# Sharing the buffers of the early modulation transfers group by group, and queueing the later modulation's loads behind them

## The chip, the cores and the metric

The kernel runs on one core of one Trainium2 chip. The metric is the device time of one execution in microseconds (us). The kernel before the change was timed in three runs: 2575.25, 2576.55 and 2578.53, median 2576.55. One further execution was recorded by the profiler.

## The reference: what is computed

The reference is a backbone of two layers over 512 latent tokens and 256 context tokens, with 2048 features and everything in float32. Cut to what matters here:

```
for l in (0, 1):
    mod  = silu(c)     @ w_mod[l] + b_mod[l]      # shift, scale, gate of the latents, 3 x 2048
    cmod = silu(c_ctx) @ w_mod[l] + b_mod[l]      # the same for the context
    h  = rmsnorm(x,  norm_g[l]) * (1 + scale)  + shift
    hc = rmsnorm(cx, norm_g[l]) * (1 + cscale) + cshift
    u, uc = h @ w_in[l], hc @ w_in[l]             # all mixer columns and the gate path
    y  = concat(mixer 1, mixer 2) * silu(gate columns)
    x  = x + gate * (y @ w_o[l])                  # the context likewise in layer 0
out = rmsnorm(x, final_g)
```

Layer 0 mixes with differential attention (A) and windowed attention (B), layer 1 with two others. The modulation is a product of two vectors (c and c_ctx) with a matrix of 48 MB for each layer. Nothing of layer 0 can start before the shift and the scale for its first features are known; the gate of layer 0 and all of the modulation of layer 1 are needed much later.

## The kernel before, in words

The features lie in 16 chunks of 128, k = 0 to 15. One tile holds one chunk of all 768 tokens (`[128, 768]`, float32). The kernel text goes through a scheduler that decides the order on each engine from dependences and costs, so an engine's order isn't the order of the text.

**The start.** The 16 tiles of x are loaded (`xT`), and their common root mean square is `rs0` (a tile `e`). Then comes a loop over eight groups g = 0 to 7, each for two chunks:

- `mod_first(g)` (lines 134 to 153) computes shift and scale for chunks 2g and 2g+1. It loads 4 MB of `wm0[g]` in 11 tiles `mraw0`, ten of 384 KB and one of 256 KB (L140, on SyncE's DMA queue SP). 32 small fp32 matmuls accumulate in a PSUM tile `T` (L144), each with 32 rows of the result. ScalarE copies `T` to `e` (L149), four tiny matmuls with `sel` transpose it (L151), and `mod_finish` (DVE, L125 and L129) adds bias and gain into `modc`.
- `make_h` (L345 to L361) then makes `h` and its remainder `l` for both chunks: `xn` = xT times rs0 (L348, on GpSimd for two chunks of three, otherwise VectorE), `h` by ScalarE (L353), `xn` again and `l` by VectorE (L356, L218). Each float32 value is split in two parts, and three passes of matmuls h·wh, l·wh and h·wl (L278, L279, L281) stand for one product.
- For each chunk four start columns of the input projection (one head's key, query and value of mixer A, and one gate column) are accumulated: 4 columns × 3 passes × (512 latent and 256 context columns) = 24 matmuls. Below, H0 to H15 are these 24 matmuls of the chunks 0 to 15. While the matmuls of group g stand in the text, those of `mod_first(g+1)` are interleaved with them. The weights of the start columns come every fourth chunk: three `wraw` tiles and one in the slot of `macc` (L268), each split to `wh` (ScalarE, L259) and `wl` (VectorE, L218).

**Where the 88 modulation tiles live.** `hslot` takes one of the 32 slots of pool `hT`, which the 32 tiles h and l fill in the end. `slot` takes one of the 11 slots of pool `s3`, in which `sil` (the stationary operand of the modulation matmuls) and xT[2] to xT[11] live; such a slot comes free when an xT tile has been used by `make_h`. Before the change groups 0 to 4 take `hT` and groups 5 to 7 take `s3`:

```
raw = hslot("mraw0", F32) if g < 5 else slot("mraw0")
```

A load waits until its slot is free. All loads stand in one queue on SP, in an order fixed in advance: a load that waits holds up everything behind it.

**The later modulation.** `mod_later` (L155 to L185) computes four chunks of the rest (block b) from eight tiles `mraw` of 512 KB, in two buffers (L163). For each half tile and each of the two vectors VectorE accumulates (L173: macc += mraw·silc, for c), or ScalarE multiplies in place (L170) and GpSimd adds (L171, for c_ctx). So an eight-tile block has 15 of L173 on VectorE, and 15 of L171 on GpSimd. The generator `later()` goes through twelve blocks with two vectors and then four with one; `tick` draws from it as projections proceed. Its first block is b = 8 of layer 0. Its loads carry no order of their own, except those of the last four blocks, which are issued behind `last_x`.

**After the start.** `load_cs(64)` loads the rotation tables cos and sin (L336), behind the last early load (`last_raw`). The value column goes through `ev` (ScalarE, L447 and L448) to a transpose on TensorE (L453); key and query are copied to `r` (ScalarE, L411 and L413), rotated (`rope`: VectorE L401 and L402, GpSimd L403 and L404) and split (L218: kl, qa, qb). The next projections have weights `wraw` of 512 KB, split into two `wh`/`wl` each; the first of them is the key column of the next head, whose result is copied to an `r` as well (called r_1950 in the order below). wl_1977 belongs to the projection after it.

Of the kernel before, what the change touches and what calls it, by code (L numbers as in the profile page):

```python
# [9 lines left out]
F32 = mybir.dt.float32  # L10
# [7 lines left out]
P = 128  # L18
# [23 lines left out]
def trunk_kernel(ctx: ExitStack, tc: tile.TileContext, T):  # L42
# [5 lines left out]
    wp = ctx.enter_context(tc.tile_pool(name="wp", bufs=4))  # L48
# [16 lines left out]
    def slot(name):  # L65
        return sp["s3"].tile([P, TOK], F32, tag="s3", name=name)
# [13 lines left out]
    def hslot(name, dt=F32R):  # L80
        return hp.tile([P, TOK], dt, tag="hT", name=name)
# [40 lines left out]
    def mod_finish(l, k0, nk, src, nv=2):  # L122

        dst = modc[l][:, k0:k0 + nk, 0:nv]
        nc.vector.tensor_tensor(dst, src, bmod[:, 48 * l + k0:48 * l + k0 + nk].unsqueeze(2).broadcast_to([P, nk, nv]),  # L125
                                op=ALU.add)
        if NCH <= k0 < 2 * NCH:
            g0 = V_NG + 16 * l + k0 - NCH
            nc.vector.scalar_tensor_tensor(dst, dst, 1.0, vcol[:, g0:g0 + nk].unsqueeze(2).broadcast_to([P, nk, nv]),  # L129
                                           op0=ALU.add, op1=ALU.mult)  # L130

    last_raw = [None]

    def mod_first(g):

        acc = pst.tile([P, 512], F32, name="T")
        for r0 in range(0, 32, 3):
            n = min(3, 32 - r0)
            raw = hslot("mraw0", F32) if g < 5 else slot("mraw0")
            last_raw[0] = nc.sync.dma_start(raw[:, :n * 256], T["wm0"][g][:, r0 * 256:(r0 + n) * 256])  # L140
            for i in range(n):
                sec, at = divmod(r0 + i, NCH)
                j = at % 4
                nc.tensor.matmul(acc[32 * j:32 * j + 32, 256 * sec:256 * sec + 256], lhsT=sil[:, at, :],  # L144
                                 rhs=raw[:, 256 * i:256 * i + 256], start=(at < 4), stop=(at >= NCH - 4),
                                 tile_position=(0, 32 * j))
            yield
        asb = sp["ep"].tile([P, TOK], F32, name="e")[:, 0:512]
        nc.scalar.copy(asb, acc)  # L149
        for i in range(4):  # L150
            nc.tensor.matmul(acc[:, 2 * i:2 * i + 2], lhsT=asb[:, P * i:P * i + P], rhs=sel, start=True, stop=True)  # L151
        for sec in range(2):
            mod_finish(0, 2 * g + NCH * (1 - sec), 2, acc[:, 4 * sec:4 * sec + 4].rearrange("p (c v) -> p c v", c=2))
        yield

    def mod_later(l, b, nv, behind=None):

        macc = sm.tile([P, 2, 512], F32, name="macc", bufs=1)
        for r in range(8):
            raw = wp.tile([P, 1024], F32, name="mraw", bufs=2)  # L160
            rv = raw.rearrange("p (k c) -> p k c", k=2)
            with tc.issue_after(behind.ins) if behind is not None else nullcontext():
                nc.sync.dma_start(raw, T["wm1"][b + 4 if l else b - 8, r])  # L163
            for i in range(2):
                for v in range(nv):
                    sc = silc[:, 16 * v + 2 * r + i:16 * v + 2 * r + i + 1]
                    if r == 0 and i == 0:
                        nc.scalar.mul(macc[:, v, :], rv[:, i, :], sc)
                    elif v == 1:
                        nc.scalar.mul(rv[:, i, :], rv[:, i, :], sc)  # L170
                        nc.gpsimd.tensor_tensor(macc[:, v, :], macc[:, v, :], rv[:, i, :], op=ALU.add)  # L171
                    else:
                        nc.vector.scalar_tensor_tensor(macc[:, v, :], rv[:, i, :], sc, macc[:, v, :],  # L173
                                                       op0=ALU.mult, op1=ALU.add)
            if r < 7:
                yield
        mp = psj.tile([P, 512], F32, name="J")
        for i in range(4):
            for v in range(nv):
                at = 4 * i + 2 * v  # L180
                nc.tensor.matmul(mp[:, at:at + 2], lhsT=macc[:, v, 128 * i:128 * i + 128],  # L181
                                 rhs=ones[:, 0:2], start=True, stop=True)
        mod_finish(l, 4 * b, 4, mp[:, 0:16].rearrange("p (a v o) -> p a v o", v=2, o=2)[:, :, 0:nv, 0], nv)
        yield
# [13 lines left out]

    def later():
        for b in range(8, 12):  # L200
            yield from mod_later(0, b, 2)
        for b in (4, 5, 6, 7, 0, 1, 2, 3):
            yield from mod_later(1, b, 2)
        for b in range(8, 12):
            yield from mod_later(1, b, 1, last_x)

    bg = later()
    due = [0.0, 0]

# [165 lines left out]
    for _ in mod_first(0):  # L375
        pass
    for g in range(NCH // 2):
# [3 lines left out]
        for k in (2 * g, 2 * g + 1):  # L381
            for i, (lat, cx) in enumerate(start_ps):
                if k % 4 == 0:
                    raw = sm.tile([P, 2, 512], F32, name="macc", bufs=1).rearrange("p a b -> p (a b)") if i == 3 else None
# [657 lines left out]
```

## Time and profile before

| what | value |
|---|---|
| three runs, median (lowest to highest) | 2576.55 us (2575.25 to 2578.53) |
| the profiled execution's own time | 2573.45 us |
| its span in the profile | 2571.7 us |
| mean granted TensorE clock | 0.977 |
| PE busy | 2427.3 us, 94% of the span |
| DVE / ACT / POOL busy | 63% / 44% / 20% |
| 384 KB modulation loads | 80, median 7.3 us from issue to landing |

In the views, PE is TensorE, DVE is VectorE, ACT is ScalarE, POOL is GpSimd, and SPq is SyncE's DMA queue. Timeline rows read: start in us, duration in us, engine, line, operation, out<-in, shapes, count, and in brackets the idle time before with what ended it. Rows of waits read: waiting engine, tile and line, what it waited for, us in total, times, longest. Rows of windows read: from:to, length, then busy us (and instructions) of PE, PEld, DVE, ACT and POOL, the granted TensorE clock, the DMA share and GB/s.

### The profile page before, as it was taken

The numbers are of one execution on the slowest core, as the hardware profiler recorded it, in microseconds if no ns is written. First come the engines' busy times: TensorE is split into PE (matmuls) and PEld (weight loads), VectorE is DVE, ScalarE is ACT, GpSimd is POOL, SyncE is SP. The second block draws the span as 40 slices with busy tenths as digits, with TensorE's granted clock in tenths as the row PEclk, the third lists the DMA queues.
The fourth block names the chain that finished last, engine by engine and source line by source line (L and its number), as shares of the span: only waits on it lengthen the run. The fifth ranks groups of instructions, "written<-read, shape, count | busy, mean of one in ns | idle before, by whom it ended". The sixth has DMA issues, their size and how long they took to land.

```text
span 2571.7 us, 36748 instructions
## 1 busy us (share of the span) xinstructions
PE 2427.3 (94%) x14214; PEld 2088.3 (81%) x14214; DVE 1608.2 (63%) x2720; ACT 1128.6 (44%) x2143; POOL 517.6 (20%) x340
## 2 busy tenths in 40 slices
PE   4889999999999999999999999899999999999998
PEld 2667888988788888878878888688888888887787
DVE  4367666656865787877666554857735325776534
ACT  3244444544554554544343332444434334554434
POOL 1132001101400354353303442310010001000010
PEclk9899999999999999999999999899999999999999
DMA  9762111111312233342334554535522222222234
GB/s 326 251 216 74 48 50 56 56 55 57 105 53 69 90 133 124 107 145 97 118 127 153 183 182 138 205 106 170 178 70 79 78 83 70 62 87 70 92 117 148
DMA packets 99087, 297.51 MB, mean 116 GB/s; under 512 B 11616, under 2 KB 12640, under 8 KB 98912
## 3 DMA queue, kind: packets, MB, share of 16 engines
q1 hardware_dynamic: 98912, 295.16, 34.5%
q8 instruction: 112, 1.84, 0.3%
q14 instruction: 63, 0.52, 0.1%
HBM read 269.16 MB, written 25.95 MB: 115 GB/s over the span
## 4 chain that ended last, share of the span: by engine, by line
PE 51%; DVE 7%; issue 2%; ACT 2%; DMA 2%; POOL 1%; ACTq 0%; SPq 0%; DVEq 0%; POOLq 0%
PE J L278 13%; PE J L279 13%; PE J L281 13%; PE O L533 4%; PE S L477 2%; DVE macc L173 2%; PE T L518 2%; DMA mraw<-in_wm_dram 2%; PE S L473 2%; DVE wl L218 1%; POOL macc L171 1%; DVE l L359 1%; DVE mc L489 1%; PE J L181 1%; PE T L243 0%
## 5 line engine op out<-in xcount | busy, mean ns | idle before, releaser
L278 PE MATMUL J<-h,wh 128*128 128x512 f32 (+1 forms) x2224 | 791.3, 359 | 23.8 <-ACT h L353 13.4
L279 PE MATMUL J<-l,wh 128*128 128x512 f32 (+1 forms) x2224 | 769.0, 356 | 4.7 <-DVE l L359 2.7
L281 PE MATMUL J<-h,wl 128*128 128x512 f32 (+1 forms) x2224 | 709.1, 356 | 2.8 <-DVE wl L218 2.8
L218 DVE TENSOR_TENSOR wl<-wraw,wh 128x512 fp32r<-128x512 f32 x500 | 402.2, 809 | 348.2 <-ACT wh L259 326.6
L259 ACT CAST wh<-wraw 128x512 fp32r<-128x512 f32 x492 | 302.4, 618 | 545.2 <-PE J L279 472.1
L278 PEld LDWEIGHTS J<-h,wh 128*128 128x128 f32 x2224 | 424.7, 192 | 104.7 <-ACT h L353 14.5
L279 PEld LDWEIGHTS J<-l,wh 128*128 128x128 f32 x2224 | 426.1, 192 | 62.6 <-DVE l L218 3.9
L281 PEld LDWEIGHTS J<-h,wl 128*128 128x128 f32 x2224 | 390.6, 192 | 38.8 <-DVE wl L218 5.1
L171 POOL TENSOR_TENSOR macc<-macc,mraw 128x512 f32<-128x512 f32 x180 | 267.9, 1489 | 254.1 <-ACT mraw L170 226.6
L278 PE MATMUL J<-yh,wh 128*128 128x512 f32 (+1 forms) x800 | 276.6, 352 | 5.1 <-ACT yh L441 5.1
L279 PE MATMUL J<-yl,wh 128*128 128x512 f32 (+1 forms) x800 | 272.8, 351 | 1.0 <-DVE yl L218 0.9
L173 DVE SCALAR_TENSOR_TENSOR macc<-mraw,silc,macc 128x512 f32<-128x512 f32 x240 | 241.7, 1007 | 42.3 <-DMA mraw<-in_wm_dram 38.6
L281 PE MATMUL J<-yh,wl 128*128 128x512 f32 (+1 forms) x800 | 253.2, 350 | 0.0
L489 DVE TENSOR_REDUCE mc<-S 128x1 f32<-128x768 f32 (+3 forms) x208 | 166.1, 799 | 137.9 <-PE S L477 88.1
L170 ACT ACTIVATE mraw<-mraw,silc 128x512 f32<-128x512 f32 x180 | 129.4, 723 | 192.4 <-DVE macc L173 171.6
L522 ACT CAST pth<-T 128x256 fp32r<-128x256 f32 (+2 forms) x288 | 124.9, 450 | 160.6 <-PE T L518 157.3
L278 PEld LDWEIGHTS J<-yh,wh 128*128 128x128 f32 x800 | 150.9, 190 | 32.8 <-ACT yh L441 5.9
L279 PEld LDWEIGHTS J<-yl,wh 128*128 128x128 f32 x800 | 151.1, 189 | 22.1 <-DVE yl L218 2.8
L218 DVE TENSOR_TENSOR ptl<-T,pth 128x256 fp32r<-128x256 f32 (+2 forms) x288 | 144.5, 514 | 38.6 <-ACT pth L522 35.1
L498 ACT ACTIVATE e<-S,nb 128x256 f32<-128x256 f32 (+3 forms) x144 | 104.3, 724 | 145.1 <-DVE nb L494 102.2
L281 PEld LDWEIGHTS J<-yh,wl 128*128 128x128 f32 x800 | 140.6, 190 | 12.4
L403 POOL TENSOR_TENSOR r<-r,cos 128x512 f32<-128x512 f32 x31 | 44.3, 1429 | 476.3 <-DVE t L402 361.4
(287 smaller groups left out, 3424.7 us busy)
## 6 DMA issues: line engine op xcount, KB each, us to landing
mraw<-in_wm_dram SPq DMA_DIRECT2D x128, 512.0 KB, 3.7
wraw<-in_ew_dram SPq DMA_DIRECT2D x96, 512.0 KB, 3.6
wraw<-in_ow_dram SPq DMA_DIRECT2D x64, 512.0 KB, 3.6
wraw<-in_wo_dram SPq DMA_DIRECT2D x62, 512.0 KB, 3.8
mraw<-in_wm_dram SPq DMA_DIRECT2D x80, 384.0 KB, 7.3
xT<-in_xT_dram SPq DMA_DIRECT2D x16, 384.0 KB, 7.8
res<-in_xT_dram SPq DMA_DIRECT2D x16, 384.0 KB, 4.4
xad<-nx SPq DMA_DIRECT2D x16, 384.0 KB, 2.3
```

The lines of the kernel that those rows point to most:

```text
L170: nc.scalar.mul(rv[:, i, :], rv[:, i, :], sc)
L171: nc.gpsimd.tensor_tensor(macc[:, v, :], macc[:, v, :], rv[:, i, :], op=ALU.add)
L173: nc.vector.scalar_tensor_tensor(macc[:, v, :], rv[:, i, :], sc, macc[:, v, :], op0=ALU.mult, op1=ALU.add)
L218: nc.vector.tensor_tensor(o, a, h.bitcast(F32), op=ALU.subtract)
L259: nc.scalar.copy(wh[:, :n, :], rv[:, k0:k0 + n, :])
L278: nc.tensor.matmul(o, lhsT=wh, rhs=xh[:, c0:c1], start=first and (opens or o is lat), stop=False)
L279: nc.tensor.matmul(o, lhsT=wh, rhs=xl[:, c0:c1], start=False, stop=False)
L281: nc.tensor.matmul(o, lhsT=wl, rhs=xh[:, c0:c1], start=False, stop=last and (closes or o is lat))
L489: nc.vector.reduce_max(mc, S, axis=AX.X)
L498: nc.scalar.activation(e, S, AF.Exp, bias=nb, scale=scale, accum_out=den)
L522: nc.scalar.copy(ph, tv)
L533: nc.tensor.matmul(o, lhsT=v[:, cols[i]], rhs=pt[part][:, i, :], start=(n == 0), stop=(n == len(steps) - 1))
```

## The change

`mod_first` no longer decides by the group alone. The first 11, 11, 11, 11, 11, 6, 4 and 3 tiles of groups 0 to 7 take `hT`, the rest take `s3`, and the last two tiles of group 7 take the two `mraw` buffers of the later modulation. The later modulation's blocks 8 to 11 of layer 0 and 0 to 7 of layer 1 get `last_raw[0]`, the last early load, as the load behind which theirs are issued. Behind the edit at line 139 all line numbers grow by 7: L144 is L151 then, L151 is L158, L163 is L170, L173 is L180, L218 is L225, L268 is L275, L278 is L285.

```
-            raw = hslot("mraw0", F32) if g < 5 else slot("mraw0")
+
+            i = r0 // 3
+            if i < (11, 11, 11, 11, 11, 6, 4, 3)[g]:
+                raw = hslot("mraw0", F32)
+            elif g == 7 and i > 8:
+                raw = wp.tile([P, 1024], F32, name="mraw", bufs=2)
+            else:
+                raw = slot("mraw0")
             last_raw[0] = nc.sync.dma_start(raw[:, :n * 256], T["wm0"][g][:, r0 * 256:(r0 + n) * 256])
...
         for b in range(8, 12):
-            yield from mod_later(0, b, 2)
+            yield from mod_later(0, b, 2, last_raw[0])
         for b in (4, 5, 6, 7, 0, 1, 2, 3):
-            yield from mod_later(1, b, 2)
+            yield from mod_later(1, b, 2, last_raw[0])
```

The number behind a tile's name tells the instance. Tiles mraw_832 to mraw_912 are group 4's, mraw_968 to mraw_1066 group 5's, mraw_1116 to mraw_1196 group 6's, mraw_1252 to mraw_1350 group 7's.

TensorE, at the end of group 4's modulation matmuls, before:

```order
L144 MATMUL T<-mraw_853,sil 32x256 x3
L144 MATMUL T<-mraw_968,sil 32x256 x3
L144 MATMUL T<-mraw_973,sil 32x256
L144 MATMUL T<-mraw_864,sil 32x256 x3
L144 MATMUL T<-mraw_973,sil 32x256 x2
L144 MATMUL T<-mraw_990,sil 32x256
L144 MATMUL T<-mraw_869,sil 32x256 x3
L144 MATMUL T<-mraw_990,sil 32x256 x2
L144 MATMUL T<-mraw_995,sil 32x256 x3
...
L144 MATMUL T<-mraw_912,sil 32x256 x2
L144 MATMUL T<-mraw_1050,sil 32x256 x3
L151 MATMUL T<-sel,e 128x2 x4
```

The same place now, with the first rows of H8 behind it:

```order
L151 MATMUL T<-mraw_853,sil 32x256 x3
L151 MATMUL T<-mraw_864,sil 32x256 x3
L151 MATMUL T<-mraw_869,sil 32x256 x3
L151 MATMUL T<-mraw_880,sil 32x256 x3
L151 MATMUL T<-mraw_885,sil 32x256 x3
L151 MATMUL T<-mraw_896,sil 32x256 x3
L151 MATMUL T<-mraw_901,sil 32x256 x3
L151 MATMUL T<-mraw_912,sil 32x256 x2
L158 MATMUL T<-sel,e 128x2 x4
L285 MATMUL J<-h_8_945,wh 128x512 x3
```

Group 5's matmuls, 27 of which stood among group 4's and the other five in the first rows of H8, have left this place.

TensorE, around the start of H10 (chunk 10, the first of group 5), before:

```order
L281 MATMUL O<-h_9_954,wl 128x512
L281 MATMUL S<-h_9_954,wl 128x256
L144 MATMUL T<-mraw_1116,sil 32x256 x3
L144 MATMUL T<-mraw_1121,sil 32x256 x3
L278 MATMUL J<-h_10_1099,wh 128x512
```

And now:

```order
L288 MATMUL O<-h_9_954,wl 128x512
L288 MATMUL S<-h_9_954,wl 128x256
L151 MATMUL T<-mraw_1017,sil 32x256 x3
L151 MATMUL T<-mraw_1034,sil 32x256 x3
L151 MATMUL T<-mraw_1039,sil 32x256 x3
L151 MATMUL T<-mraw_1050,sil 32x256 x3
L151 MATMUL T<-mraw_1055,sil 32x256 x3
L151 MATMUL T<-mraw_1066,sil 32x256 x2
L158 MATMUL T<-sel,e 128x2 x4
L285 MATMUL J<-h_10_1099,wh 128x512 x3
```

Group 5's own matmuls, 15 of them among H9's and 17 behind H9, and its `sel` now stand directly ahead of H10; before, its `sel` was inside H9, and group 6's matmuls stood here. In the same way group 7's matmuls, 30 of which stood ahead of H12, now stand at the end of H13, with `sel` directly ahead of H14, and group 6's stand inside H11, with `sel` ahead of H12.

VectorE, from the last early `l` tile (l0_15, chunk 15) to the first rotation, before (macc_2241 belongs to the later modulation's first block, whose tiles are mraw_2242, 2833, 3552, 3971, 4563, 4840, 5566 and 6151):

```order
L173 SCALAR_TENSOR_TENSOR macc_2241<-mraw_4563,silc_181,macc_2241 128x512
L218 TENSOR_TENSOR l0_15_1393<-xn_1390,h0_15_1392 128x768
L173 SCALAR_TENSOR_TENSOR macc_2241<-mraw_4840,silc_181,macc_2241 128x512 x2
L218 TENSOR_TENSOR wl_1837<-wraw_1834,wh_1836 128x512
L401 TENSOR_TENSOR t2_1454<-r_1451,sin64_1449 32x512
```

And now:

```order
L180 SCALAR_TENSOR_TENSOR macc_2241<-mraw_2833,silc_181,macc_2241 128x512
L225 TENSOR_TENSOR l0_15_1393<-xn_1390,h0_15_1392 128x768
L180 SCALAR_TENSOR_TENSOR macc_2241<-mraw_3552,silc_181,macc_2241 128x512
L225 TENSOR_TENSOR wl_1837<-wraw_1834,wh_1836 128x512
L180 SCALAR_TENSOR_TENSOR macc_2241<-mraw_3552,silc_181,macc_2241 128x512
L408 TENSOR_TENSOR t2_1454<-r_1451,sin64_1449 32x512
```

At the first rotation the block stands at its sixth tile of eight before (11 of 15 L173 done), and at its third now (5 of 15 done). Between the first rotation and wl_1977 four L173 stood before (tiles 5566 and 6151); seven stand there now (tiles 3971, 4563, 4840 and the first of 5566).

SP, at the end of the early loads, before: behind group 7's last tile mraw_1350 come cos, sin and six loads of the later modulation; two of its loads stand far ahead, behind the first four weight loads. Now:

```order
L275 DMA macc<-in_ew_dram 128x512
L147 DMA mraw<-in_wm_dram 128x768
L147 DMA mraw<-in_wm_dram 128x512
L343 DMA cos_1447<-in_cos_dram 128x512
L343 DMA sin_1449<-in_sin_dram 128x512
L147 DMA mraw_1034<-in_wm_dram 128x768
```

This is the place of the two early loads of the later modulation: group 7's last two tiles and the tables have taken it. All eight loads of the first later block now stand behind mraw_1274, group 7's third tile, which has become the last early load of the queue.

## The prediction

> **What bounds the kernel now.** I read the page first, then the windows of the first 300 us, then TensorE's timeline there, then those of VectorE and SP. The page says who is the bottleneck:
>
> ```profile
> span 2571.7 us, 36748 instructions
> PE 2427.3 (94%) x14214; PEld 2088.3 (81%) x14214; DVE 1608.2 (63%) x2720; ACT 1128.6 (44%) x2143; POOL 517.6 (20%) x340
> ```
>
> TensorE is idle for 144 us in all. The change touches loads and work of about the first 230 us, so I look at its windows there (PE's busy us is the second number, DVE's the fourth, POOL's the sixth, then clock, DMA share, GB/s):
>
> ```profile
> 105.00:110.00 5.00, 3.82 (x13) 3.15 (x14) 4.05 (x10) 2.50 (x4) 0.00 (x0) 0.66 0.00 0
> 129.00:137.00 8.00, 7.52 (x30) 4.66 (x29) 5.61 (x7) 1.79 (x4) 1.98 (x1) 0.57 1.03 400
> 145.00:160.00 15.00, 15.00 (x108) 9.35 (x108) 4.06 (x6) 3.23 (x6) 2.02 (x2) 1.00 0.90 309
> 160.00:187.00 27.00, 22.78 (x163) 17.59 (x163) 24.09 (x30) 14.83 (x24) 16.38 (x11) 1.00 0.48 152
> 187.00:207.00 20.00, 13.93 (x55) 10.58 (x54) 19.74 (x18) 13.17 (x22) 10.88 (x7) 0.91 0.34 107
> 207.00:222.00 15.00, 11.48 (x70) 11.04 (x71) 14.76 (x17) 4.67 (x8) 6.36 (x4) 0.77 0.22 71
> 222.00:300.00 78.00, 73.38 (x439) 64.90 (x438) 48.22 (x100) 34.97 (x70) 2.60 (x2) 0.98 0.16 53
> ```
>
> Three stretches stand out. From 145 to 160 TensorE has no gap at full clock. From 187 to 222 VectorE is busy 34.5 of 35 us and TensorE idles 9.6. From 222 on TensorE is busy 94% again, so what has been lost by then isn't won back: the shift at about 222 us is the forecast's shift at the end. (A measurement of this kernel tells a difference from none at about 0.2%, 5.15 us.)
>
> Now TensorE's timeline, at the starts of groups 2, 4, 5, 6 and 7 and behind H15:
>
> ```profile
> 81.27 1.92 PE L144 MATMUL T<-mraw,sil 128*32 128x256 f32 x28
> 83.87 1.05 PE L151 MATMUL T<-sel,e 128*128 128x2 f32 x8 [0.69 <-ACT e L149]
> 86.34 1.65 PE L278 MATMUL J<-h,wh 128*128 128x512 f32 x3 [1.42 <-ACT h L353]
> ...
> 106.18 1.22 PE L278 MATMUL J<-h,wh 128*128 128x512 f32 x2 [1.37 <-ACT h L353]
> ...
> 128.57 0.97 PE L278 MATMUL J<-h,wh 128*128 128x512 f32 x3 [1.42 <-ACT h L353]
> ...
> 143.93 0.49 PE L278 MATMUL J<-h,wh 128*128 128x512 f32 x1
> 145.23 0.63 PE L144 MATMUL T<-mraw,sil 128*32 128x256 f32 x6
> 145.79 0.51 PE L278 MATMUL J<-h,wh 128*128 128x512 f32 x1
> ...
> 160.25 3.22 PE L144 MATMUL T<-mraw,sil 128*32 128x256 f32 x52
> 163.40 0.97 PE L278 MATMUL J<-h,wh 128*128 128x512 f32 x3
> 176.35 0.96 PE L278 MATMUL J<-h,wh 128*128 128x512 f32 x3 [1.18 <-ACT h L353]
> 179.39 0.50 PE L279 MATMUL J<-l,wh 128*128 128x512 f32 x1 [1.73 <-DVE l L218]
> 186.73 0.28 PE L281 MATMUL S<-h,wl 128*128 128x256 f32 x1
> 189.53 0.66 PE L453 MATMUL J<-identr,ev 128*128 128x128 f32 x4 [2.51 <-ACT ev L447]
> 204.42 0.39 PE L281 MATMUL J<-h,wl 128*128 128x512 f32 x1
> 210.52 0.58 PE L278 MATMUL J<-h,wh 128*128 128x256 f32 x1 [5.71 <-ACT r L411]
> 218.61 0.40 PE L278 MATMUL J<-h,wh 128*128 128x512 f32 x1
> ```
>
> Between groups lies what I call a tail: from the last modulation matmul of a group (in group 2 at 83.19) over copy, `sel`, `modc` and `h` to the first H matmul (86.34), 3.15 us. It is bare in the early groups. It is covered at H10 and H12, which start without a wait (143.93, 163.40), because the modulation matmuls were done a group earlier and others stand in the tail. After the bare tails of H6 and H8 the clock is low for several us (0.66, 0.57).
>
> **The change, part by part.** The prices of TensorE's work first. From 179.39 to 187.01 run the last 43 of the 48 matmuls of H14 and H15: 7.62 us, so 8.5 for all 48 at full clock. A modulation tile (three matmuls) costs 0.56 us between H matmuls (145.23 to 145.79), and in a block one matmul costs 3.22/26 = 0.124 (52 entries are 26 matmuls, two passes each). A spell at low clock costs 8 us × (1 − 0.57) = 3.4 behind H8; behind H6 5 × (1 − 0.66) = 1.7 in that window alone. I take 2.8.
>
> *Group 4 to 5.* The loads up to group 4 keep their count ahead of them: 9 tiles in `s3` slots and the first 1 MB still come early, only others, and 0.13 MB more (under 0.4 us at 400 GB/s). The first four groups and H8's start I leave at 128.6. There, while TensorE waited for group 4's last tiles, it did 27 of group 5's 32 modulation matmuls. Now they stand among and behind H9. So this group becomes like the early ones: 8.5 (H8, H9) + 2.8 (clock) + 5 × 0.56 + 17 × 0.124 = 4.9 (modulation) + 3.15 (tail) = 19.4. Group 2's cycle, measured, is 106.18 − 86.34 = 19.84. H10 starts at 148.0 instead of 143.93: +4.0. Group 5's first six tiles are now loaded late, behind group 4's and four weight tiles; six tiles at 0.98 us from about 122 are there before H9 needs the first at about 138, so they cost nothing. That 0.98 is 384 KB at the 400 GB/s of the window 129:137.
>
> *Group 5 to 6.* 8.5 + 2.8 (a tail at H10 that wasn't bare) + 4 × 0.56 + 20 × 0.124 = 4.7 + 2.5 (`sel` to h, 83.87 to 86.34; the copy is hidden by 15 matmuls of H11) = 18.5. H12 at 166.5 instead of 163.40: +3.1.
>
> *Group 6 to 7.* 8.5 + 1.4 (half of 2.8, the tail being shorter) + 0.56 + 29 × 0.124 = 4.2 + 3.15 = 17.2. H14 at 183.7 instead of 176.35: +7.4. The load queue could hold group 7's last three tiles here, behind three weight loads of the next projection, which wait for wl (chunks 12 to 15); these are free at about H11's end, 164, and three tiles land by 170, ahead of 175.
>
> *H14 and H15.* 8.5 + 2.8 = 11.3 against 10.66, whose wait for `l` (1.73) now falls under the slower matmuls, as L173 no longer stands ahead of it. H15 ends at 195.0 instead of 187.0: **+8.0**. Ends: +3.7 if only one of the three new tails costs clock, +9.3 if all do in full.
>
> [...] The windows above show clocks of 0.66 and 0.57 after two tails of 3.15 us, in which the only work is 1.05 us of tiny matmuls. [...]
>
> *The later modulation.* Its loads were free runners before, and two landed at 43 us. Now the first is issued when group 7's last tiles are used, about 178. SP, VectorE and GpSimd before:
>
> ```profile
> 33.39 1.31 SPq L163 DMA_DIRECT2D mraw<-in_wm_dram  x2
> ...
> SPq L163 <- POOL macc L171: 38.7, 8, 11.4
> ```
>
> ```profile
> 187.01 1.75 DVE L218 TENSOR_TENSOR wl<-wraw,wh 128x512 fp32r<-128x512 f32 x1 [1.30 <-PE S L281]
> 191.59 0.69 DVE L218 TENSOR_TENSOR wl<-wraw,wh 128x512 fp32r<-128x512 f32 x1
> 208.48 0.75 DVE L173 SCALAR_TENSOR_TENSOR macc<-mraw,silc,macc 128x512 f32<-128x512 f32 x1
> 209.27 0.95 DVE L218 TENSOR_TENSOR qa<-r,qa 64x768 fp32r<-64x768 f32 x1
> 218.09 2.40 DVE L218 TENSOR_TENSOR wl<-wraw,wh 128x512 fp32r<-128x512 f32 x2
> ```
>
> The same subtraction takes 0.69 us alone and 1.75 beside a GpSimd operation: each GpSimd tile costs VectorE about 1.06. From H15's end to wl_1977 (187.0 to 218.1) VectorE works 31.1 us without a break, with four L173 and eight GpSimd operations. In the new order seven L173 stand there, and about eleven GpSimd operations: 3 × 0.75 + 3 × 1.06 = +5.4. In return VectorE is freed of eight L173 before H15's end, where I have counted that already (the wait for `l`). How much of the 5.4 reaches TensorE: before, it resumed at 210.52 and needed 8.1 us to 218.61, when wl_1977 was just coming. In the new order the first scores stand ahead of those matmuls and wait for qa. Qa comes 22.3 to 25 us after H15's end, then 8.1 us: 30.4 to 33.1 after H15's end, against 31.6 before, so −1.2 to +1.5 by this path; by wl_1977 up to +5.4. I take **+2**, nearer to the first path, since TensorE's 8.1 us of matmuls run while VectorE does what stands behind qa.
>
> The 5.71 us that TensorE waited for `r` don't come off this sum: the copy stood behind a multiplication for the last of the eight tiles on ScalarE, and stands behind one for the fifth now, so this wait may go; but qa is awaited in its place, at nearly the same distance from H15's end.
>
> *Moved tables.* cos and sin (512 KB) come early and are in the 0.13 MB above. Nothing more.
>
> Behind 230 us the order differs in places of two or three rows; I price it at 0 ± 3.
>
> Sum: 8.0 + 2 = +10 on the profiled execution's 2573.45 (span 2571.7, 1.75 around it), 2583.5; the median of the runs lies 3.1 above that execution, so **2586.5**.
>
> **The rivals.**
>
> *No change.* TensorE's waits behind H15 (2.51 and 5.71, and the low clock after the second: 0.77 over 15 us, 3.4) swallow the loss. If VectorE keeps up, TensorE goes from H15's end at 195.0 through 17.8 us of matmuls (187.0 to 204.81, with its first wait) to 212.8, and on at full clock, against 210.52: +2.3, less some 2 for the clock: about 0, 2577. For: ScalarE's copy of `r` stands behind fewer tiles. Against: VectorE is busy 98% in 187 to 222, and gets more there. Chance 0.19.
>
> *The clock holds.* [...] For: H14's gap of 1.18 us left it at 1.00 (160 to 187). Against: the two rows above. Chance 0.05.
>
> *Faster.* VectorE, relieved of eight L173 between 160 and 187, gives h and l sooner; the clock holds at H12 and H14 (H15's end +3.7), and the loads of the later modulation fall late enough that VectorE's chain doesn't grow: less 5.71 and 3.4 behind H15: −5.4, 2571. It decides at about 210: TensorE must not wait there. Against: qa. Chance 0.14.
>
> *Much slower.* The later tiles land behind each other (SP waited 38.7 us in eight waits for GpSimd), and weight loads stand behind them in the queue: two waits of the mean, 4.8 each, on top: about +20, 2596. Chance 0.07.
>
> **How the numbers follow.** The forecast (+5.2 to +14) has 0.55. Slower by over 0.2%: 0.55 + 0.07 = 0.62. Within: 0.19 + 0.05 = 0.24. Faster: 0.14. The range leaves out the faster case's lower part and the much slower case's upper: 2573 to 2596. It takes in the ends of H15 (+3.7 to +9.3) with the ends of the VectorE chain (−1.2 to +5.4) and ± 3 behind: 2576 to 2594.
>
> **What would show it.** In the new profile: H8 at 128.6, H10 at 148, H12 at 166.5, H14 at 184, H15's end at 195, each with clock below 0.8 in the 5 us behind; then a wait of TensorE for qa at about 204 to 219, and the match of 218.61 at about 229. I am wrong if H10 starts before 146 (then group 4's cover wasn't worth what I think), or if TensorE has no wait over 2 us between 195 and 225 (then the loss was swallowed).

## The result, and the profile after

| | before | after |
|---|---|---|
| median (lowest to highest), four runs each | 2575.90 us (2571.75 to 2578.53) | 2595.92 us (2593.62 to 2597.11) |
| profiled execution, its span | 2573.45, 2571.7 | 2595.23, 2593.5 |

The ratio is 1.0078, 95% interval 1.0061 to 1.0096: slower by 20.0 us, where +10 was forecast. In a later series (17 runs of before, six of after) the same two kernels stood at 2572.70 and 2589.42, ratio 1.0069, interval 1.0054 to 1.0083: +16.7.

The page of the kernel after, in its first lines:

```profile
span 2593.5 us, 36751 instructions
PE 2433.7 (94%) x14214; PEld 2095.1 (81%) x14214; DVE 1607.9 (62%) x2720; ACT 1128.9 (44%) x2143; POOL 517.3 (20%) x340
```

The same 14214 matmuls were busy 6.4 us longer (the mean granted clock was 0.975 instead of 0.977), and TensorE idled 159.8 us instead of 144.4: 15.4 more. Its timeline shows where the idle time lies. These are its entries at the starts of H8, H10, H12 and H14 and behind H15:

```profile
124.28 1.05 PE L158 MATMUL T<-sel,e 128*128 128x2 f32 x8 [0.74 <-ACT e L156]
126.75 1.13 PE L285 MATMUL J<-h,wh 128*128 128x512 f32 x3 [1.42 <-ACT h L360]
...
144.05 1.05 PE L158 MATMUL T<-sel,e 128*128 128x2 f32 x8 [0.73 <-ACT e L156]
146.52 0.97 PE L285 MATMUL J<-h,wh 128*128 128x512 f32 x3 [1.42 <-ACT h L360]
...
163.32 0.96 PE L285 MATMUL J<-h,wh 128*128 128x512 f32 x3 [1.41 <-ACT h L360]
...
181.82 1.50 PE L285 MATMUL J<-h,wh 128*128 128x512 f32 x3 [1.42 <-ACT h L360]
...
192.65 0.28 PE L288 MATMUL S<-h,wl 128*128 128x256 f32 x1
193.94 0.66 PE L460 MATMUL J<-identr,ev 128*128 128x128 f32 x4 [1.00 <-ACT ev L454]
...
205.44 0.50 PE L288 MATMUL J<-h,wl 128*128 128x512 f32 x1 [1.70 <-DVE wl L225]
...
219.17 0.58 PE L480 MATMUL S<-kh,qa 128*128 128x256 f32 x1 [8.45 <-DVE qa L225]
...
226.93 0.40 PE L285 MATMUL J<-h,wh 128*128 128x512 f32 x1
...
230.91 0.62 PE L288 MATMUL J<-h,wl 128*128 128x512 f32 x2 [2.29 <-DVE wl L225]
```

H10 and H12, which started without a wait, now wait 1.42 and 1.41 us for `h`, at the end of a tail. H15 ends at 192.93 instead of 187.01. The wait of 5.71 for `r` is gone; 8.45 for qa has come, and then 2.29 for wl.

The windows of the same stretch (busy us and count of PE, PEld, DVE, ACT, POOL, then clock, DMA share, GB/s):

```profile
126.70:131.70 5.00, 4.78 (x17) 3.71 (x18) 4.90 (x6) 1.70 (x3) 2.00 (x1) 0.66 0.91 349
131.70:136.70 5.00, 5.00 (x34) 3.33 (x32) 1.18 (x2) 0.00 (x0) 0.00 (x0) 1.00 0.40 132
146.50:151.50 5.00, 4.36 (x15) 3.52 (x16) 4.93 (x6) 1.67 (x3) 2.01 (x1) 0.66 0.98 355
163.30:168.30 5.00, 4.35 (x15) 3.51 (x16) 4.48 (x7) 1.67 (x3) 0.00 (x0) 0.66 0.92 339
181.80:186.80 5.00, 4.98 (x18) 4.05 (x19) 4.97 (x8) 4.22 (x7) 1.35 (x2) 0.66 0.15 61
192.90:218.20 25.30, 13.83 (x55) 10.58 (x54) 24.94 (x22) 14.19 (x23) 15.51 (x10) 0.82 0.32 99
218.20:231.00 12.80, 9.21 (x57) 8.72 (x57) 12.63 (x15) 5.29 (x11) 7.00 (x5) 0.81 0.23 78
```

Behind each tail the clock is 0.66 over the next five us (for 3.41 of them the trace has 0.50), and then 0.99 or 1.00; the second trace of this kernel (after_again, below) has 0.66 or 0.67 behind all four as well. From H15's end to the start of qa VectorE is busy 24.94 of 25.30 us: it is the bound there. Before, the matching stretches were these:

```profile
187.01:209.30 22.29, 13.92 (x55) 10.58 (x54) 21.96 (x21) 13.19 (x23) 10.87 (x7) 0.90 0.35 114
209.30:222.00 12.70, 11.48 (x70) 11.04 (x71) 12.53 (x14) 4.63 (x8) 6.36 (x4) 0.77 0.18 52
```

POOL had 7 and then 4 operations there, and has 10 and 5 now. VectorE's timeline of the kernel after shows some of the later modulation's operations there (L180 is the old L173) and the two results that TensorE waits for:

```profile
198.10 1.76 DVE L180 SCALAR_TENSOR_TENSOR macc<-mraw,silc,macc 128x512 f32<-128x512 f32 x1
...
207.00 2.56 DVE L180 SCALAR_TENSOR_TENSOR macc<-mraw,silc,macc 128x512 f32<-128x512 f32 x2
...
218.17 0.95 DVE L225 TENSOR_TENSOR qa<-r,qa 64x768 fp32r<-64x768 f32 x1
...
220.13 0.75 DVE L180 SCALAR_TENSOR_TENSOR macc<-mraw,silc,macc 128x512 f32<-128x512 f32 x1
...
229.10 3.44 DVE L225 TENSOR_TENSOR wl<-wraw,wh 128x512 fp32r<-128x512 f32 x2
```

From H15's end to the start of wl_1977 it works 36.2 us (192.93 to 229.10), and before 31.1. The match of the old 218.61 stands at 226.93, and TensorE's next matmul with wl at 230.91.

### The profile page after: what moved, and what is told of

Its sections match the earlier page's. It is cut to its first block, busy times and chain, and to the rows that moved or that the text cites. A ratio compares the mean times of both kernels' runs of the same rounds, so it can differ in the third digit from the quotient of the medians.

```text
span 2593.5 us, 36751 instructions
## 1 busy us (share of the span) xinstructions
PE 2433.7 (94%) x14214; PEld 2095.1 (81%) x14214; DVE 1607.9 (62%) x2720; ACT 1128.9 (44%) x2143; POOL 517.3 (20%) x340
## 5 line engine op out<-in xcount | busy, mean ns | idle before, releaser
L285 PE MATMUL J<-h,wh 128*128 128x512 f32 (+1 forms) x2224 | 788.8, 358 | 21.2 <-ACT h L360 15.9
L225 DVE TENSOR_TENSOR wl<-wraw,wh 128x512 fp32r<-128x512 f32 x500 | 398.4, 801 | 340.4 <-ACT wh L266 314.8
L285 PEld LDWEIGHTS J<-h,wh 128*128 128x128 f32 x2224 | 423.9, 191 | 99.6 <-ACT h L360 16.8
L285 PE MATMUL J<-yh,wh 128*128 128x512 f32 (+1 forms) x800 | 276.3, 351 | 5.2 <-ACT yh L448 5.2
L180 DVE SCALAR_TENSOR_TENSOR macc<-mraw,silc,macc 128x512 f32<-128x512 f32 x240 | 247.3, 1030 | 49.4 <-DMA mraw<-in_wm_dram 45.4
L285 PEld LDWEIGHTS J<-yh,wh 128*128 128x128 f32 x800 | 150.7, 189 | 32.8 <-ACT yh L448 6.0
L225 DVE TENSOR_TENSOR ptl<-T,pth 128x256 fp32r<-128x256 f32 (+2 forms) x288 | 144.8, 515 | 39.9 <-ACT pth L529 36.2
L286 PEld LDWEIGHTS J<-yl,wh 128*128 128x128 f32 x800 | 151.1, 189 | 22.5 <-DVE yl L225 3.3
L288 PEld LDWEIGHTS J<-yh,wl 128*128 128x128 f32 x800 | 140.7, 190 | 12.6
```

The source lines that it names most:

```text
L225: nc.vector.tensor_tensor(o, a, h.bitcast(F32), op=ALU.subtract)
L285: nc.tensor.matmul(o, lhsT=wh, rhs=xh[:, c0:c1], start=first and (opens or o is lat), stop=False)
L286: nc.tensor.matmul(o, lhsT=wh, rhs=xl[:, c0:c1], start=False, stop=False)
L288: nc.tensor.matmul(o, lhsT=wl, rhs=xh[:, c0:c1], start=False, stop=last and (closes or o is lat))
```

## The experiments

The prediction's account: the places of the early transfers make the tails (about 8 us at H15's end), and the loads queued behind them lengthen VectorE's chain a little. One rival: the queueing is the larger part, because the first later block (b = 8 of layer 0, "block 8" below) loses a stretch in which it cost little. A second rival: the order of the load queue costs far behind the start. All ratios are against before in the same series.

One measure serves all runs. The trace lists each matmul with its columns; I take the time at which TensorE had done as many columns as in the first trace of before at time t, minus t. The table also has H15's end itself. It leaves out after_warm, whose added matmuls change the columns.

| kernel | H15's end | at 240 | at 400 | at 900 | at 2500 | ratio (95%) |
|---|---|---|---|---|---|---|
| before | 187.0 | 0 | 0 | 0 | 0 | |
| before_again | 183.5 | -3.5 | -3.5 | -3.6 | -5.1 | one run |
| after | 192.9 | 12.1 | 11.6 | 14.3 | 21.8 | 1.0078 (1.0061 to 1.0096) |
| after_again | 193.9 | 13.1 | 12.7 | 16.5 | 14.2 | 1.0069 (1.0054 to 1.0083) |
| queue_only | 188.6 | 7.1 | 11.8 | 12.9 | 11.6 | 1.0049 (1.0037 to 1.0062) |
| place_only | 206.9 | 14.0 | 13.6 | 16.9 | 17.9 | 1.0062 (1.0050 to 1.0075) |
| before_late8 | 183.9 | -8.9 | 9.6 | 10.7 | 12.4 | 1.0053 (1.0039 to 1.0067) |
| after_late8 | 195.2 | 2.4 | 21.0 | 22.5 | 23.4 | 1.0088 (1.0074 to 1.0101) |
| before_spread8 | 182.2 | -9.8 | -9.1 | -6.0 | -4.3 | 0.9992 (0.9983 to 1.0001) |
| after_spread8 | 191.8 | -1.9 | 1.5 | 3.9 | 4.7 | 1.0031 (1.0020 to 1.0042) |
| g5_first | 191.5 | 9.0 | 15.5 | 16.7 | 24.7 | 1.0075 (1.0060 to 1.0090) |
| before_tail2 | 184.9 | -5.4 | -5.1 | -1.7 | -3.4 | 0.9997 (0.9988 to 1.0007) |
| before_l1order | 184.3 | -2.9 | -2.8 | -3.0 | -1.4 | 1.0010 (1.0001 to 1.0020) |

### One part alone

**queue_only**, before with the second part of the change:

```diff
-            yield from mod_later(0, b, 2)
+            yield from mod_later(0, b, 2, last_raw[0])
-            yield from mod_later(1, b, 2)
+            yield from mod_later(1, b, 2, last_raw[0])
```

> Only the second part of the change: the old places of the early tiles (groups 0 to 4 in hT, 5 to 7 in s3), but the later modulation's loads queued behind the last early load. In its order group 5's modulation matmuls stand among group 4's again, and group 6's sel and group 7's matmuls are spread over H9 to H13, as before; six L173 stand between the first rotation and wl_1977 (four before, seven in the changed kernel). Theory (two costs that add: bare tails of groups 5 to 7 before H15's end, then VectorE's longer list to wl_1977): H15 ends at 185 to 188, wl_1977 2 to 4 us later than before, and the whole run is 0 to +5 us against before. Rival A (the queueing alone is the cost, the places nothing): +15 to +20 us. Rival B (the places alone are the cost): 0 +- 3 us and no later wl_1977.

Measured: 2585.29 against 2573.84, +11.4: above the theory's range and below rival A's. H10 and H12 keep their covers. Ahead of H14 TensorE waits 2.16 us instead of 1.18, and the clock behind it is 0.50 for 6.8 us. H15 ends 1.6 us later than in before's first trace. Then two long waits follow on TensorE, and a third much later:

```profile
210.07 0.39 PE L278 MATMUL J<-h,wh 128*128 128x256 f32 x1 [3.62 <-ACT r L411]
...
224.67 1.01 PE L281 MATMUL J<-h,wl 128*128 128x512 f32 x2 [5.25 <-DVE wl L218]
...
384.38 0.58 PE L473 MATMUL S<-kh,qb 128*128 128x256 f32 x1 [4.63 <-ACT e L498]
```

The matmul that waits 5.25 us for wl had no wait in before (219.31). From H15's end to 240 this kernel loses 5.5 us more, with no tail in that stretch: the prediction's +2 for the queueing was too small. The wait of 4.63 for ScalarE's `e` at 384 belongs to another stretch. It stands in the traces of g5_first, before_late8 and after_late8 too (4.6 us each), and in neither of the two traces of before nor the two of after. These four kernels lose 6 to 7 us on before from 340 to 400; why `e` comes late in their orders wasn't followed.

**place_only**, after's table for the slots, without the branch that puts group 7's last tiles into the later modulation's buffers, and without the queueing (shown against after):

```diff
-            elif g == 7 and i > 8:
-                raw = wp.tile([P, 1024], F32, name="mraw", bufs=2)
...
-            yield from mod_later(0, b, 2, last_raw[0])
+            yield from mod_later(0, b, 2)
-            yield from mod_later(1, b, 2, last_raw[0])
+            yield from mod_later(1, b, 2)
```

> Only the first part: the new sharing of hT and s3 (group 7's last two tiles in s3, as the later modulation keeps its two buffers and its own early loads). In its order the modulation matmuls of groups 5 to 7 stand as in the changed kernel, at the end of H9, H11 and H13, and no L173 is left between the first rotation and wl_1977. Theory: H15 ends 5 to 8 us later than before, but VectorE's list behind it is shorter than before by four L173 and some six GpSimd operations, so that the wait of 5.7 us before the context matmuls goes: shift at 230 us -2 to +3, whole run -3 to +5 us. Rival A (the queueing alone): 0. Rival B (the places alone): +12 us or more at 230 us, and +15 to +20 at the end.

Measured: 2590.38 against 2573.84, +16.5. That is the number of rival B, but not its mechanism: H15 ends at 206.9, 14 later than in after. H8 already starts 3.6 us later (130.31 instead of 126.75; TensorE waits longer for its modulation tiles). The rest comes from H12 on, where 14 of block 8's 15 L173 stand ahead of the last `l` tile on VectorE. VectorE waits for block 8's loads four times on the way (8.7 us in all):

```profile
167.11 1.11 PE L283 MATMUL J<-h,wh 128*128 128x512 f32 x3 [2.37 <-ACT h L358]
...
171.77 0.79 PE L284 MATMUL J<-l,wh 128*128 128x512 f32 x1 [2.91 <-DVE l L223]
...
190.88 1.65 PE L283 MATMUL J<-h,wh 128*128 128x512 f32 x3 [3.28 <-ACT h L358]
...
197.12 0.80 PE L284 MATMUL J<-l,wh 128*128 128x512 f32 x1 [3.95 <-DVE l L223]
```

Of these 14 us, 12 are back by 240 (14.0 there against 12.1 in after): the work that stood ahead of H15 doesn't stand behind it. The two parts don't add: by 240 they cost 7.1 and 14.0, and both together 12.1. Both move the same work of block 8 about the same narrow stretch.

### Without the first later block at the start

To see the places without that collision, block 8 is taken out of the start in both orders.

**before_late8 and after_late8**: all loads of block 8 are issued behind the weight load last recorded when its step is drawn (the same edit in both; after has `last_raw[0]` for the other blocks):

```diff
+    last_w = [None]
...
-            yield from mod_later(0, b, 2)
+            yield from mod_later(0, b, 2, last_w[0] if b == 8 else None)
...
-        nc.sync.dma_start(raw[:, :nk * P], w[col // P][:, k0 * P:(k0 + nk) * P])
+        last_w[0] = nc.sync.dma_start(raw[:, :nk * P], w[col // P][:, k0 * P:(k0 + nk) * P])
```

> The kernel before, with the same late first block of the later modulation and nothing else. Theory: H15 ends 1 to 3 us earlier than before (no L173 ahead of the l tiles), the waits of 2.5 and 5.7 us behind it shrink to under 2 in all, so the shift at 230 us is -6 to -10, and the whole run is -10 to -2 us, faster than both kernels. Rival (the work of the block costs the same wherever it stands): 0 +- 3 us.

> The changed kernel, with the first later block's loads held back further, behind the last weight load that stands ahead of it in the text (in head 1), so that no L173 stands ahead of wl_1977; the places as in the changed kernel. Theory: H15's end as in the changed kernel (+5 to +6 on before), no wait for qa (8.4 us in the changed kernel) nor for wl_1977 (2.3): shift at 230 us -3 to +2, at the end -2 to +8 by what the order does at the start of layer 1. Rival (VectorE isn't what makes TensorE wait there, but the late start itself): shift at 230 us stays at +10 to +12.

Measured: 2585.88 and 2595.98 against 2573.84. By 230 us before_late8 is ahead by 9.5. Then the whole block comes in one stretch, and TensorE loses 12 us there. The window of before_late8:

```profile
230.00:260.00 30.00, 22.86 (x125) 19.73 (x124) 26.46 (x38) 16.77 (x31) 17.63 (x12) 0.88 0.36 125
```

And of before:

```profile
230.00:260.00 30.00, 30.00 (x184) 26.52 (x183) 18.09 (x40) 14.25 (x29) 2.60 (x2) 1.00 0.16 56
```

Twelve GpSimd operations instead of two, VectorE at 88% instead of 60%, and 59 matmuls fewer. What was meant to take the block's cost away put it elsewhere, so both forecasts for the whole run missed (-10 to -2 and -2 to +8). The forecasts at 230 held, and they settle a rival: after_late8 has the places of after, but no wait for qa or wl_1977, and its shift at 230 is 1.6 where after has 11.5. So it is block 8's work that TensorE waited for behind H15, and not the late start. The medians of the two runs are 10.1 apart.

**before_spread8 and after_spread8**: each of block 8's loads behind the latest weight load, so that one step at a time falls into heads 1 to 6. `last_w` is now a list to which each weight load is appended, and `mod_later` has:

```diff
+            if l == 0 and b == 8:
+                behind = last_w[-1]
```

> The kernel before, with each of the eight loads of the first later block held back behind the weight load that stands ahead of it in the text, so that its steps are spread over the heads 1 to 6 of mixer A, one at a time. With the whole block in head 1 the run gained 9.5 us up to 230 us and lost 12 at 240 to 260 and 6 more by 400. Theory (the loss comes from GpSimd's and VectorE's work of the block in a row beside the attention): the gain of 9 to 10 us at 230 stays, each step of two L173 and two L171 costs 0 to 1.5 us, whole run -9 to +2 us. Rival (the work costs TensorE the same wherever it is not beside the start): +5 to +12 us.

> The changed kernel with the same spreading of the first later block. Beside the run of the kernel before with it, this gives the price of the places alone, with no later work of VectorE at the start. Theory: H15 ends 10 to 12 us after that other run's, and that distance stays to the end (with +-3 for the order at the start of layer 1, whose queue is here the changed kernel's: then +15 to +18). Against the kernel before +1 to +9, by the step costs. Rival (bare tails are taken up by waits that go): distance of under 3 us.

Measured: 2571.13 and 2580.52 against 2572.64. TensorE's rows at the value column, before_spread8:

```profile
182.67 0.66 PE L456 MATMUL J<-identr,ev 128*128 128x128 f32 x4 [0.44 <-ACT ev L450]
```

and after_spread8:

```profile
192.01 0.66 PE L463 MATMUL J<-identr,ev 128*128 128x128 f32 x4 [0.20 <-ACT ev L457]
```

They are 9.3 us apart, the medians 9.4. Without block 8 in the way, **the places cost 9.4 us**, and what they cost at H15 arrives at the end. Two limits: the pair differs in the queueing of the blocks behind block 8 too, whose work starts only behind 630 us; and with block 8 moved the scheduler puts group 6's `sel` nine us earlier than in before's first trace, so this is the price of the places in a slightly different order.

The same pair prices block 8. Against before_spread8, which has no block 8 at the start, the two traces of before are 9.8 and 6.3 us behind at 240; against after_spread8, the two of after are 14.0 and 15.0 behind. So by 240 the block costs 6 to 10 in its old place and 14 to 15 queued behind: 4 to 9 more. Spread out it costs an estimated 5.5 to 6.6, if all that the two runs give back between 240 and 2500 is its work (-9.8 to -4.3, and -1.9 to 4.7).

**g5_first**: after, with group 5's tiles shared out the other way: its first five take `s3` slots and its last six `hT`, where in after its first six take `hT`:

```diff
-            if i < (11, 11, 11, 11, 11, 6, 4, 3)[g]:
+            if (i > 4 if g == 5 else i < (11, 11, 11, 11, 11, 6, 4, 3)[g]):
```

> The changed kernel, except that of group 5 the first five tiles take s3 and the last six hT, so that the tiles that are loaded early are those that its matmuls need first; in its order 15 of group 5's 32 matmuls stand among group 4's again. Theory (matmuls that cover TensorE's wait for group 4's last tiles are worth their time; the bare tail ahead of H10 stays): H10 starts 1.5 to 3 us earlier than in the changed kernel's 146.5, H15's end by as much, and the run is 0 to 4 us below the changed kernel's, +16 to +20 on before, with the same 6 us at the start of layer 1, where its queue has the changed kernel's order. Rival (tail and clock set the group, not the matmuls): H10 within 1 us of 146.5.

Measured: 2592.63 against 2572.64, ratio 1.0075; after has 1.0078 and 1.0069. TensorE reaches H10 3.8 us sooner than in after, though the tail is still there:

```profile
142.69 1.16 PE L285 MATMUL J<-h,wh 128*128 128x512 f32 x3 [1.42 <-ACT h L360]
```

At H12 2.3 are left (161.00), at H15's end 1.5, and at 240 it is 3.1 ahead of after. So the matmuls that cover the wait for group 4's last tiles are worth time, more than the theory had. At 400 it is 3.9 behind after: the wait for `e` described under queue_only lies between, so the run ended no faster.

### The clock in the tails

**after_warm**: after, with four more matmuls of 256 columns behind `sel` from group 4 on. Nothing uses their result:

```diff
+        for i in range(4 if g > 3 else 0):
+            nc.tensor.matmul(acc[:, 256:512], lhsT=asb[:, P * i:P * i + P], rhs=asb[:, 0:256], start=True, stop=True)
```

> The changed kernel with four additional matmuls (256 columns, their result is used by nobody) behind sel in the tails of groups 4 to 7, so that TensorE isn't idle while modc and h are made. Theory (the bare tails ahead of H10, H12 and H14 cost time also by the low clock that follows them): the clock stays above 0.9 behind those tails, each group from 5 on is 1 to 2.8 us shorter, H15 ends 3 to 8 us earlier than the changed kernel's 192.9, and the run is -8 to 0 us against the changed kernel (+12 to +20 on before). Rival (the clock falls for another reason, or the low clock hides under other waits): H15's end within 1 us of 192.9.

Measured: 2603.94 against 2572.70, ratio 1.0123 (1.0108 to 1.0137). The windows behind H8, H10 and H12:

```profile
130.70:135.70 5.00, 4.30 (x23) 3.52 (x24) 4.87 (x6) 1.72 (x4) 2.01 (x1) 1.00 0.68 269
151.40:156.40 5.00, 4.31 (x23) 3.55 (x24) 4.88 (x6) 1.71 (x4) 2.02 (x1) 1.00 0.96 374
170.10:175.10 5.00, 4.35 (x23) 3.59 (x24) 4.47 (x7) 1.66 (x3) 0.00 (x0) 1.00 0.69 261
```

The clock is 1.00 where it was 0.66, with 23 matmuls instead of 15 to 17. Ahead of H14 it is otherwise. TensorE idled 3.52 us behind the added matmuls, and the clock behind fell:

```profile
191.15 1.20 PE L287 MATMUL J<-h,wh 128*128 128x512 f32 x3 [3.52 <-ACT h L362]
```

The window behind it:

```profile
192.00:197.00 5.00, 2.76 (x8) 1.96 (x8) 4.97 (x7) 1.74 (x4) 1.95 (x2) 0.50 0.65 202
```

So the work in the tail bears on the clock behind it: low behind eight of eight tails in the two traces of after, and full behind three of four here. It is one execution. A spell costs at most 5 × (1 - 0.66) = 1.7 us of TensorE's work, but this run doesn't show that the time can be won: the forecast of a shorter run missed. `modc` now waits for the added matmuls, so TensorE needs 4.30 us from `sel` to `h` instead of 2.47 at H8, which alone takes back the 1.7. The cycles from H8 to H10 and from H10 to H12 are 20.7 and 18.7 us, instead of 19.8 and 16.8. Ahead of H14 VectorE's order differs too: block 8's first accumulation, which waited for ScalarE's first product, stands ahead of the last `modc` (L182 is the old L173). The waits of VectorE between 120 and 192 us:

```profile
DVE modc L125 <- PE T L160: 24.5, 3, 13.2
DVE macc L182 <- ACT macc L177: 13.4, 1, 13.4
```

H15 ends at 204.3, where 185 to 190 was forecast.

### Behind the start

**before_l1order** puts three loads of block 8 of layer 1 behind weight loads, which gives SP at the start of layer 1 the order that it has in after. There, the first trace of after lost 6 us between 1660 and 1720:

```diff
+            if l == 1 and b == 8 and r in (4, 6, 7):
+                behind = last_w[{4: -2, 6: -1, 7: -6}[r]]
```

> The kernel before, in which only three loads of the last later blocks at the start of layer 1 (near 1660 us) are queued behind the weight loads that stand ahead of them in the changed kernel's queue; TensorE's and VectorE's own orders hardly move. In the changed kernel TensorE falls back by another 6 us at this place. Theory (the order of SP's queue there does it): no shift up to 1650 us, +4 to +6 behind 1720, whole run +4 to +6. Rival (the places of matmuls and VectorE's order there, or the moment at which the place is reached): 0 +- 1.5 us at 1720.

Measured: 2576.03 against 2572.64, ratio 1.0010 (1.0001 to 1.0020). In its trace it loses 0.9 us to before_again between 1660 and 1720, so that order isn't what cost after 6 us there. Where its 3.4 us on the median come from stays open.

**after_again and before_again** are the two kernels unchanged, for a second trace of each.

> The changed kernel once more, for a second trace. In the first, TensorE had fallen back by 12 us at 240 us and by another 10 from there to the end, in steps near 650, 1320 and 1690 us (2, 2 and 6). Theory (the later steps come from the order that the scheduler chose there, so they recur): 11 to 13 at 240, and 8 to 11 more by the end. Rival (scatter of single executions): the steps fall elsewhere or change sign, and the run is +12 to +16 on before.

> The kernel before once more, for a second trace, to see how far two executions of one order lie apart stage by stage. Theory: up to +-3 us at 130 us (the moment at which the clock changes in the start), and within +-2 of that behind. Rival (the first trace was a lucky one behind 300 us): +4 us or more between 300 us and the end.

Measured: after_again 2589.42 (2585.94 to 2598.07) against 2572.70, before_again 2568.38 in one run. The step of 6 us at 1660 to 1720 is 2.3 in after_again, and 2.2 in before_again against the first trace of before. From 240 to 2500 after_again loses 1.1 us, where the theory had 8 to 11 by the end. So most of that step belonged to one execution and not to the kernel. The two traces of before differ by 3.5 us from 150 us on, with the same instructions in the same order. TensorE in before_again:

```profile
127.51 0.96 PE L278 MATMUL J<-h,wh 128*128 128x512 f32 x3 [1.42 <-ACT h L353]
...
140.45 0.49 PE L278 MATMUL J<-h,wh 128*128 128x512 f32 x1
```

H8 to H10 is 12.9 us here and 15.4 in the first trace. The clock of 129 to 137 was 1.00 here:

```profile
129.00:137.00 8.00, 7.49 (x49) 5.89 (x50) 4.95 (x8) 0.92 (x3) 1.99 (x1) 1.00 1.02 399
```

It was 0.57 in the first. In before_l1order, whose TensorE order is the same, the eight us from 126 have 0.57 too, and in before_tail2, the same up to H15, the low spell is half as long. So behind one and the same tail the clock was 0.50 for 6.8, 6.8, 3.4 and 0 us in four executions. The 3.4 us that I took as a price is the upper end of that scatter.

**before_tail2**: before, with only the last two loads of block 8 behind the latest weight load (`r > 5`), as a version that might beat both.

```diff
+            if l == 0 and b == 8 and r > 5:
+                behind = last_w[-1]
```

> The kernel before, in which only the last two of the first later block's eight loads are held back behind weight loads of later heads, so that the four L173 and four L171 that stood between H15's end and wl_1977 are gone from there; the order of H0 to H15 and of all modulation matmuls is unchanged. Theory (VectorE's list sets TensorE's start of the projection behind the first head): H15's end as before, the match of 218.61 comes 4 to 7 us earlier, and the whole run is -7 to -1 us. Rival (that list isn't the bound; TensorE waits as long for something else): 0 +- 1 us at 230 us.

Measured: 2572.61 against 2572.70, ratio 0.9997 (0.9988 to 1.0007). The long wait behind H15 becomes shorter, 3.97 instead of 5.71:

```profile
205.63 0.39 PE L281 MATMUL J<-h,wh 128*128 128x256 f32 x1 [3.97 <-DVE vl L221]
```

From H15's end to 220 us 3.2 us are won. The shift at 230 is -5.3 against before's first trace, but only -1.8 against before_again. The whole run isn't faster as forecast: some 3.9 us are given back, near 630 to 690 and at 880. The two tiles' work on VectorE stands at 543 to 590, so why they are given back isn't shown. Neither this nor before_spread8 beats before by more than their intervals.

## Why the prediction was right in sign and half in size

I set the mean of the two traces of each kernel against each other, since one trace of before can be 3.5 us off. At H15's end the difference is 193.4 - 185.3 = 8.2 us; from there to 240 it is 6.2 (12.6 + 1.75 = 14.35 in all); behind 240 another 6.2 (18.0 + 2.55 = 20.55 at 2500). The prediction had 8.0, 2, and 0 ± 3.

*The places, +8.0: right.* The four cycles from H8 to H15's end were forecast at 19.4, 18.5, 17.2 and 11.3, 66.4 in all. They measured 19.8, 16.8, 18.5 and 11.1 in the trace after, 66.2 in all. The tails came where they were expected, and each is followed by a low clock. The pair without block 8 agrees, with 9.4, and so do the two further traces with before's order up to H15 (before_l1order 184.3, before_tail2 184.9): with them the difference is 8.5. H10, at 146.5 and 147.3, is behind the 146 below which the prediction would have been wrong.

That the sum comes out so well is partly luck, since errors in it cancel. *The low clock* was priced at 2.8 for a tail; it is 1.7 in after (five us at 0.66, then 1.00), and it follows H12's shorter tail in full, where half was taken. By that the four spells cost 6.8 us instead of the 9.8 in the sum, so some 3 us lie elsewhere in the four cycles; where isn't shown. H10 to H12 took 1.7 less than forecast, H12 to H14 1.3 more. And before's first trace, the base of the sum, has the longest of the low spells behind H8's tail. H8 itself came at 126.75 and 127.40 instead of 128.6; before_again has it at 127.51 too.

Tails of at most 3.21 us in the trace after (at H8 from 123.54 to 126.75), with 0.95 to 1.05 us of two-column matmuls in them, were followed by a low clock in all four cases, 0.66 over five us each, and so were the four in after_again, at 0.66 or 0.67. In three of the four traces with before's order the tail ahead of H8 was followed by one too; in before it took 2.47 us from `sel` on (126.10 to 128.57), behind three of group 5's matmuls, and not 3.15. Four matmuls of 256 columns behind `sel` went with a clock of 1.00 in three cases of four.

*VectorE's chain, +2: the step that failed.* The parts were counted nearly rightly: seven L173 stand between H15's end and wl_1977, where four stood before; GpSimd has 10 and 5 operations in the two windows, against 7 and 4 (four more, where three were counted). One count is off, but cost little: VectorE is freed of six L173 before H15's end (eleven stood there, five do now), and not of eight, and TensorE still waits 0.55 us for an `l` at 189.51. VectorE's chain from H15's end to wl_1977 grew by 36.2 - 31.1 = 5.1, where the prediction had +5.4 as its upper end. But it took a value near the path by qa, which it put at 22.3 to 25 us behind H15's end. The work on qa starts 25.2 us behind it and is done at 219.12, 26.2 behind; the 0.95 us of the work itself had been left out. By that path alone the loss is 2.4 (26.2 + 7.8 = 34.0 to the match of 218.61, against 31.6). Then TensorE waits for wl_1977 as well (2.29), and the loss is 11.6 - 5.9 = 5.7 behind that. The reason given for the +2, that TensorE's matmuls run while VectorE does what stands behind qa, doesn't hold: from qa to the start of wl_1977 VectorE needs 10.0 us (219.12 to 229.10), where it needed 7.9 (210.22 to 218.09). The path that I had kept as the far end decided. Why each tile costs more than its own 0.75 us is seen in VectorE's rows: in after the accumulation takes 0.75 us at 220.13, with GpSimd idle, and 1.76 at 198.10, beside a GpSimd operation that runs from 197.54 to 199.32.

*The wait for `r`: right.* The 5.71 us went, and qa took its place, with 8.45.

*Behind 230 us, 0 ± 3: too narrow.* Traces of the same order differ by 7.6 us at their ends (21.8 and 14.2). Of the 6.2 us there, about two recur at 650 to 700 in both traces of after; the rest differs between executions. Its cause isn't shown. The 5 to 7 us that queue_only and g5_first lose between 240 and 400 go with the wait of 4.6 us for `e`, which after doesn't have.

*The rivals.* "No change" needed TensorE to come through at about 212.8; it waited for qa until 219.17, because VectorE had no slack. "The clock holds" (an estimate: the 10 less the 7.0 of clock priced for the three new tails, so +3) fell with the windows at 0.66 behind all four tails. "Faster" decided at about 210, where TensorE must not wait. "Much slower" had the right time, 2596, by a mechanism that isn't there. SP's waits for GpSimd in the trace after:

```profile
SPq L170 <- POOL macc L178: 32.1, 7, 8.1
```

They are 32.1 us in seven waits, and were 38.7 in eight. What is lost between H15's end and 240 us comes from VectorE and not from the load queue: the waits for qa and wl_1977 end on VectorE, and after_late8 hasn't got them. So "much slower" had its number by luck.

## What to carry to other kernels

A load that comes early is worth what its work covers. TensorE did most of group 5's modulation matmuls while it waited for group 4's last tiles, and to give the early places to other groups' tiles cost 9.4 us, though no byte more was loaded in all. Background work on VectorE and GpSimd must be costed against the engine that bounds the stretch it lands in: block 8 cost 6 to 10 us beside the start, 14 to 15 when pushed to where TensorE waits for VectorE, and 12 or more in one piece in a stretch where TensorE had been gapless. And before a spell of low clock or a shift of a few us becomes a price, a second trace of the same kernel shows whether it recurs.

## What the runs showed of the hardware

- In both traces of after the granted clock was 0.66 or 0.67 over the five us behind each of the four tails, 1.7 us of full clock. Four matmuls of two columns stand in these tails and didn't prevent it. With four of 256 columns added it was 1.00 behind three of the four; behind the last, where TensorE also idled 3.52 us, it was 0.50.
- Behind one and the same tail the low clock didn't come every time: behind H8's tail the spell at 0.50 lasted 6.8 us in before and before_l1order, 3.4 in before_tail2, and was absent in before_again, on the same order of TensorE's work.
- Two executions of one kernel on the same order were 3.5 us apart after 150 us (before), and two of another 7.6 us apart at 2500 (after). That is as large as most of the effects studied here, and it limits what one trace can say.
